# A one-core RWKV-7 / HGRN2 / pooling block: queue places of the solver, of the transpositions and of the first weights, five staging buffers for the output weights, and another order of the last HGRN steps

## The chip, the cores and the metric

The program runs on one core of a Trainium2 chip. It computes one layer of a hybrid backbone over 2048 latent tokens and 256 context tokens, all in float32. The metric is the device time of one execution in microseconds (us), from the kernel's first to its last instruction; times of a kernel are the median of its runs.

The engines are PE (TensorE, matrix products), DVE (VectorE), ACT (ScalarE), POOL (GpSimd) and SP (SyncE, which here only issues DMAs). Each engine takes its instructions in one fixed order. An instruction whose input is not there holds everything behind it on that engine.

## The reference, cut to what matters

```python
p_lat = (_layer_norm(h_x) * (1.0 + sc_l[:, None]) + sh_l[:, None]) @ w_in[l]
p_ctx = (_layer_norm(h_ctx) * (1.0 + sc_c) + sh_c) @ w_in[l]
pv_l, u_l, fh_l, g_l = _split_proj(p_lat)
...
y_rc, y_rl = _rwkv_branch(u_c, u_l, ...)
o_hc, o_hl = _hgrn_branch(fh_c, fh_l, ...)
pool_l = _pool_branch(pv_l, True, pool_w[l], pool_scale[l])
mix_l = jnp.concatenate([pool_l, y_rl, o_hl], axis=-1) * jax.nn.silu(g_l)
new_x = _layer_norm(ALPHA * h_x + gt_l[:, None] * (mix_l @ w_out[l])) * ln_g[l] + ln_b[l]
```

RWKV is a recurrence over tokens in two directions (the state is multiplied by a decay, loses its part along one key and gains an outer product). HGRN is a gated recurrence over tokens in two directions. Each branch is gated by SiLU of its own part of the input projection; the output projection merges them.

## The kernel before, in words

**Stages.** First come the layer norm and the projections that RWKV needs (until about 490 us). Then three things run one behind the other, with the remaining input projections threaded through them as filler for PE: RWKV (about 550 to 1335 us), HGRN (about 1335 to 1834 us) and the readout with the output projection (to the end).

**The filler** is the generator `filler` (lines 537 to 593). For each of three parts of 768 tokens it loads the activations `fxs`/`fxl` (line 542), splits them into a high and a low half (`split`, lines 213 and 214: a cast on ACT to `fxh`, a subtraction on DVE to `fxl`), and then goes over 22 blocks of 128 output columns. For each block `weights` (line 563) loads 512 KB into `fwf` (line 217, one buffer, SP's queue), casts it on ACT to `fwh` (line 213) and subtracts on POOL to `fwl` (line 214). 24 matmuls per group of tokens (line 583) follow: eight of (fxh, fwh), eight of (fxh, fwl), eight of (fxl, fwh). A group's `sink` takes the result away; its second half (`rest`: for the pooling blocks the product of line 642) is run inside the next group, after its 18th matmul (line 587).

**RWKV** goes over 36 chunks of 64 tokens in both directions. Chunk n's triangular systems are set up by `start` (matmuls of line 738, masks of line 740 on DVE), collected by `gather` (lines 778 to 780), and solved for four chunks together by `solve` (lines 784 to 803): 31 pairs of a multiplication (line 795, tile `tm`) and a subtraction (line 798, tile `o`), all on DVE. `merge` (lines 822 to 861) fetches the solution (`nn`, `at`), transposes it on DVE (lines 839 and 842) and multiplies on PE (line 847). `step` does the recurrence itself; its new state `zbd` is made on DVE by lines 903 (`tz`) and 905 from the matmuls of line 899. So DVE has four kinds of work in one queue: masks, transpositions, states, and the solver. The order on PE is written by hand in the loop of lines 960 to 991 (under `manual_schedule`); the order on the other engines, SP's queue among them, is set by a scheduler from that program.

**HGRN** goes over windows of 256 tokens, one of context and eight of latents, with a slot table (line 1167). In window n the *levels* of window n (line 1061 on PE, line 1090 on DVE for `qp` and on POOL for `ks`) alternate with the *steps* of window n−1 (lines 1120, 1123, 1133 on PE, and the state `sbd` by line 1138 on DVE, six of it per step). After the last levels one window holds steps alone. The weights of the output projection are loaded there too (`out_weights`, lines 1146 to 1158): eight pieces of 384 KB into the one `fwf`, multiplied on POOL by the gate (line 1153), cast on ACT, subtracted on DVE (line 214).

**The readout** (lines 1231 to 1287) loads `ya`, `yb`, `oa`, `ob` and, for the pooled channels, `gt` and `mx` (lines 1236 to 1255), adds on POOL (lines 1251 and 1259), multiplies `mx` on DVE (line 1256), splits it into `mh` (ACT, line 1243) and `ml`, and normalises `ya` by a chain of DVE and ACT operations (lines 1261 to 1265). PE's output projection starts with `mh` (line 1300); PE's transposes of `ya` (line 1274) come next in its order.

## Time and profile before

| what | value |
|---|---|
| median of 3 runs | 2080.55 us (2076.18 to 2083.02) |
| the profiled execution | 2072.91 us, span of its trace 2070.8 us |
| PE busy | 1835.0 us, 89% of the span |
| DVE busy | 1435.9 us, 69% |
| ACT, POOL busy | 922.4 us (45%), 796.9 us (38%) |
| chain that ended last | PE 50%, DVE 19%, DMA 7%, issue 4%, ACT 2%, POOL 2% |

The span is that of one execution. The chain that ended last is followed back from the last instruction, at each step to whatever released it. The busy shares are means over stages with different limits, so each stage is read by itself, and in it the idle time of PE and what ended it.

### The profile page before, as it was taken

How to read it: one execution, taken by the hardware profiler on the slowest of the kernel's cores; microseconds unless marked ns; L12 is line 12 of the kernel's file. 1: busy time of each engine (PE TensorE's matmuls, PEld its weight loads, DVE VectorE, ACT ScalarE, POOL GpSimd, SP SyncE). 2: the span in 40 equal slices, each digit the busy share in tenths (PEclk: the TensorE clock that was granted, in tenths of full speed). 3: DMA queues.
4: the chain of work that ended last, by engine and by line, in shares of the span. 5: the costliest groups of instructions: out<-in, count | busy, mean ns of one | idle time of the engine just before them, and what ended most of it. 6: DMA issues, size and time to landing. Idle time of an engine off the chain costs nothing.

```text
span 2070.8 us, 47037 instructions
## 1 busy us (share of the span) xinstructions
PE 1835.0 (89%) x18498; PEld 1556.3 (75%) x18498; DVE 1435.9 (69%) x3040; ACT 922.4 (45%) x1759; POOL 796.9 (38%) x735
## 2 busy tenths in 40 slices
PE   5698899994898898999988897989999999869898
PEld 2687788884786677787777786877778778758887
DVE  3778889997047857846766756258778888669863
ACT  4876777664222342332333234355456555222331
POOL 0144345655321233232223222354345553434753
PEclk8899899997899999999999999999999999659999
DMA  8444444435555576565655655443233332176632
GB/s 305 157 147 136 134 127 123 123 100 177 156 168 145 159 230 182 158 175 154 176 153 152 169 144 161 136 138 109 79 101 103 110 91 85 55 262 194 215 133 74
DMA packets 286452, 305.32 MB, mean 147 GB/s; under 512 B 85076, under 2 KB 244948, under 8 KB 285208
## 3 DMA queue, kind: packets, MB, share of 16 engines
q1 hardware_dynamic: 276072, 271.64, 43.7%
q10 hardware_dynamic: 5040, 18.09, 2.6%
q0 software_dynamic: 5120, 12.59, 1.9%
q8 instruction: 146, 2.39, 0.5%
q14 instruction: 74, 0.61, 0.1%
HBM read 205.49 MB, written 96.74 MB: 146 GB/s over the span
## 4 chain that ended last, share of the span: by engine, by line
PE 50%; DVE 19%; DMA 7%; issue 4%; ACT 2%; POOL 2%; SPq 1%; DVEq 0%; ACTq 0%; POOLq 0%
PE fps L583 18%; PE ps L332 3%; PE pa L1061 3%; PE po L1300 2%; DVE tm L795 2%; PE pa L738 2%; DVE o L798 2%; PE pa L874 2%; PE pa L1123 2%; PE pa L1120 2%; PE pa L880 2%; DVE sbd L1138 2%; PE pa L890 2%; PE po L1304 1%; PE po L1302 1%
## 5 line engine op out<-in xcount | busy, mean ns | idle before, releaser
L214 POOL TENSOR_TENSOR fwl<-fwf,fwh 128x1024 fp32r<-128x1024 f32 x66 | 158.8, 2407 | 360.7 <-ACT fwh L213 338.9
L583 PE MATMUL fps<-fxh,fwh 128*128 128x256 f32 (+1 forms) x952 | 224.7, 371 | 24.6 <-ACT fwh L213 17.0
L583 PE MATMUL fps<-fxl,fwh 128*128 128x256 f32 (+1 forms) x952 | 219.8, 364 | 1.3 <-DVE fxl L214 1.3
L583 PE MATMUL fps<-fxh,fwl 128*128 128x256 f32 (+1 forms) x952 | 212.5, 355 | 1.9 <-POOL fwl L214 1.9
L583 PEld LDWEIGHTS fps<-fxh,fwh 128*128 128x128 f32 x952 | 156.9, 197 | 54.3 <-ACT fwh L213 19.0
L583 PEld LDWEIGHTS fps<-fxl,fwh 128*128 128x128 f32 x952 | 160.7, 198 | 29.5 <-issue 5.6
L583 PEld LDWEIGHTS fps<-fxh,fwl 128*128 128x128 f32 x952 | 155.9, 193 | 28.2 <-POOL fwl L214 3.0
L1138 DVE SCALAR_TENSOR_TENSOR sbd<-sbd,tot,pa 64x64 f32<-64x64 f32 x432 | 120.6, 279 | 37.8 <-PE pa L1133 27.7
L920 POOL TENSOR_TENSOR ys<-ys,pp 64x384 f32<-64x384 f32 x64 | 75.0, 1172 | 186.2 <-ACT ys L917 176.1
L1056 ACT COPY qb<-qp 64x384 f32<-64x384 f32 x192 | 99.9, 520 | 100.4 <-PE pa L1061 67.6
L795 DVE TENSOR_TENSOR tm<-m,o 96x31 f32<-96x31 f32 (+15 forms) x279 | 114.7, 411 | 39.2 <-DMA m<-sd 31.3
L332 PE MATMUL ps<-xh,wh 128*128 128x258 f32 x768 | 129.0, 309 | 6.4 <-DVE t L337 4.4
L740 DVE TENSOR_TENSOR at<-pa,cst 128x384 f32<-128x384 f32 x144 | 74.1, 548 | 82.9 <-PE pa L738 82.3
L798 DVE TENSOR_TENSOR o<-o,tm 96x31 f32<-96x31 f32 (+15 forms) x279 | 120.4, 432 | 7.9
L332 PEld LDWEIGHTS ps<-xh,wh 128*128 128x128 f32 x768 | 108.7, 203 | 20.4 <-issue 7.8
L332 PE MATMUL ps<-xh,wl 128*128 128x258 f32 x768 | 119.7, 297 | 0.0
L1090 POOL TENSOR_TENSOR ks<-ks,tot 128x384 f32<-128x384 f32 x90 | 86.8, 969 | 84.7 <-PE pa L1061 74.2
L332 PE MATMUL ps<-xl,wh 128*128 128x258 f32 x768 | 116.4, 291 | 1.6 <-DVE xl L322 1.6
L332 PEld LDWEIGHTS ps<-xh,wl 128*128 128x128 f32 x768 | 106.8, 201 | 4.7 <-issue 4.3
L332 PEld LDWEIGHTS ps<-xl,wh 128*128 128x128 f32 x768 | 103.3, 194 | 5.1 <-issue 3.0
L1061 PE MATMUL pa<-qb,ks 128*64 128x64 f32 x2304 | 92.5, 233 | 6.9 <-POOL ks L1090 3.5
L412 POOL TENSOR_TENSOR kr<-t 128x256 f32<-128x256 f32 x54 | 47.1, 871 | 130.0 <-ACT t L399 65.1
(233 smaller groups left out, 4351.9 us busy)
## 6 DMA issues: line engine op xcount, KB each, us to landing
fwf<-in_w_in_dram SPq DMA_DIRECT2D x66, 512.0 KB, 4.4
xt<-in_x_dram ACTq DMA_DIRECT2D x32, 512.0 KB, 4.3
s_kr<-kr SPq DMA_DIRECT2D x54, 256.0 KB, 2.3
s_bk<-bk SPq DMA_DIRECT2D x54, 256.0 KB, 2.4
bks<-s_bk SPq DMA_DIRECT2D x72, 192.0 KB, 3.0
krs<-s_kr SPq DMA_DIRECT2D x72, 192.0 KB, 3.2
bk<-s_bk SPq DMA_DIRECT2D x72, 192.0 KB, 3.0
kr<-s_kr SPq DMA_DIRECT2D x72, 192.0 KB, 3.8
```

What stands on the lines that cost most here:

```text
L214: eng.tensor_tensor(out=wl, in0=wf, in1=wh.bitcast(F32), op=ALU.subtract)
L332: PE.matmul(ps[:, 0:TG + 2], a[:, k, :], b[:, k, :], start=(i == 0), stop=(i == 23))
L412: G.tensor_tensor(out=kr[:, :, pr], in0=c4(kk), in1=e_k, op=ALU.mult)
L583: PE.matmul(ps[:, 0:n], a[:, k, :], b[k][:, o:o + n], start=(i == 0), stop=(i == 23))
L740: V.tensor_tensor(out=at[:, h], in0=pa[h], in1=cst[:, C_MASK[d]].unsqueeze(1).broadcast_to([P, NPR, P]), op=ALU.mult)
L795: V.tensor_tensor(out=tv, in0=m[:, j:j + 1, j + 1:32].broadcast_to([nrow, na, nb]), in1=o[:, 0:na, j:j + 1].broadcast_to([nrow, na, nb]), ...
L798: V.tensor_tensor(out=o[:, 0:na, j + 1:32], in0=o[:, 0:na, j + 1:32], in1=tv, op=ALU.subtract)
L920: G.tensor_tensor(out=ys[vr], in0=ys[vr], in1=pp[d][vr], op=ALU.add)
L1056: S.copy(out=qb[hh, :, :, h, :].rearrange("q p c (i b) -> q (p c) i b", b=b), in_=src[hh].rearrange("q p (c i j b) -> q (p c) i j b", c=nc ...
L1061: PE.matmul(pl[64 * (c % 2):64 * (c % 2) + 64, :, p, c // 2, :], ks[:, p, CH * c:CH * c + CH], qb[:, p, c, :, :], start=True, stop=True)
L1090: eng.tensor_tensor(out=v_, in0=v_, in1=tv[:, :, :, 1 - par:2 - par].broadcast_to([P, NPR, nb, b]), op=ALU.mult)
L1138: V.scalar_tensor_tensor(out=sn[hh, p, hh], in0=so_[hh, p, hh], scalar=tot[hh, p, c:c + 1], in1=ps[hh, p, :], op0=ALU.mult, op1=ALU.add)
```

## The change

It edits the filler, the RWKV loop, the staging of the output weights and the HGRN slots. Lines shift by 1 to 13.

- `weights` leaves the loop over the parts. The first block's weights are issued ahead of the first activations, and the first weights of the second and third part are fetched at the end of the part before. `rest` runs behind all 24 matmuls of the next group, not behind the 18th.
- `gate["v"]` names the newest mask or state on DVE. Pieces of the solver and the transpositions of `merge` are put into the program with `issue_after(gate)`: the scheduler places them behind that instruction. `merge` and `solve` yield after their loads; merge's loads are put to the start of an iteration, and a solver's load to the end of the iteration that gathers its fourth chunk.
- `out_weights(0)` rotates over `fwf`, two `fwh` and two `fwl`, five buffers in all.
- In the window with steps alone the directions alternate (s0, s1, s0, s1) where before each took two in a row. In the window before it, the filler is paced to slot 7, and the output weights are run two per slot from there.

```diff
+        nxt = weights(blocks[0][0])
         xs = ahead(parts[0])
...
-                if bi + 1 < len(blocks):
-                    nxt = weights(blocks[bi + 1][0])
+                if bi + 1 < len(blocks) or pi + 1 < len(parts):
+                    nxt = weights(blocks[(bi + 1) % len(blocks)][0])
...
-                                if i == 18:
-                                    run(rest)
+                        run(rest)
                         rest = sink(fp, side["ps"], sl, n, ps[:, 0:n])
...
-                    V.tensor_tensor(out=at[:, h], in0=pa[h],
+                    gate["v"] = V.tensor_tensor(out=at[:, h], in0=pa[h],
                                     in1=cst[:, C_MASK[d]].unsqueeze(1).broadcast_to([P, NPR, P]), op=ALU.mult)
...
             G.memset(o.rearrange("q a t -> q (a t)")[:, 0:32 * 32:33], -1.0)
+            yield 1
...
                 ws[n][d]["uv"] = uv
+            yield 1
...
-                    V.tensor_tensor(out=zn[d].rearrange("q p (h e) -> q p h e", h=2), in0=tz,
+                    gate["v"] = V.tensor_tensor(out=zn[d].rearrange("q p (h e) -> q p h e", h=2), in0=tz,
...
-                            go("sol", g, solve, k)
+                            with tc.issue_after(gate["v"].ins):
+                                go("sol", g, solve, k)
                 go("stp", n, step)
                 go("late", n + 1, late)
+                go("mer", n + 1, merge)
...
-                go("mer", n + 1, merge)
+                with tc.issue_after(gate["v"].ins):
+                    go("mer", n + 1, merge)
...
+                if s_ % SB == SB - 1:
+                    go("sol", s_ // SB, solve)
                 beside(n, 0.22)
...
-                wf = fp.tile([P, KB, P], F32, name="fwf").rearrange("q k c -> q (k c)")[:, 0:n]
+                nm0, bufs, dt = (("fwf", 1, F32), ("fwh", 2, F32R), ("fwl", WB, F32R))[k % 3 if j == 0 else 0]
+                wf = fp.tile([P, KB, P], dt, name=nm0, bufs=bufs)
+                wf = (wf if dt is F32 else wf.bitcast(F32)).rearrange("q k c -> q (k c)")[:, 0:n]
...
-                for si, slot in enumerate(slots):
+                for si, slot in enumerate(slots if n < nw else slots[:4] + ("s0", "s1") * 4):
...
-                    if n < nw - 1:
+                    if n < nw - 1 or n == nw - 1 and si < 7:
                         pace(H_FIL[0] if n == 0 else H_FIL[1] if n < 3 else H_FIL[2])
                     elif n == nw - 1:
-                        run(fill if si == 0 else ow, None if si == 0 else 1)
+                        if si == 7:
+                            run(fill)
+                        run(ow, 2)
```

Three places show what the scheduler makes of it. A row is one instruction, or several alike in a row, as they stand on their engine.

The first place is SP's queue where the filler's first loads stand. Before, the first load of weights (`fwf`) comes behind the last activations (`fxs`) and four loads for RWKV:

```order
181 L542 DMA fxs<-s_x 128x256
182 L542 DMA fxs<-s_x 128x512
183 L542 DMA fxs<-s_x 128x256
184 L725 DMA bks_6005<-s_bk 128x384
185 L726 DMA krs_6004<-s_kr 128x384
186 L725 DMA bks_6010<-s_bk 128x384
187 L726 DMA krs_6009<-s_kr 128x384
188 L542 DMA fxs<-s_x 128x512
189 L217 DMA fwf<-in_w_in_dram 128x1024
190 L725 DMA bks_6253<-s_bk 128x384
```

In the change, still among the stores of the stage before (`s_kr`, `s_bk`, `s_vt`) and ahead of the first activations:

```order
147 L423 DMA s_kr<-kr 128x4x128
148 L424 DMA s_bk<-bk 128x4x128
149 L390 DMA s_vt<-t 128x2x128
150 L423 DMA s_kr<-kr 128x4x128
151 L217 DMA fwf<-in_w_in_dram 128x1024
152 L423 DMA s_kr<-kr 128x4x128
153 L424 DMA s_bk<-bk 128x4x128
154 L390 DMA s_vt<-t 128x2x128
155 L440 DMA s_bon<-t 128x256
156 L542 DMA fxs<-s_x 128x256
```

The load went up by all of the 24 loads of activations; the second load of weights now stands right behind them (its row is 185).

The second place is DVE in chunk 10, the second iteration of the solver of chunks 12 to 15. `tm` and `o` are the solver, `at` from `pa` the masks, `zbd` the state. Before, the transpositions (L842) stand ahead of this piece, and seven solver operations stand between `o` 96x18x14 and the first mask:

```order
1185 L798 TENSOR_TENSOR o<-o,tm 96x18x14
1186 L795 TENSOR_TENSOR tm<-m,o 96x247
1187 L798 TENSOR_TENSOR o<-o,tm 96x19x13
1188 L795 TENSOR_TENSOR tm<-m,o 96x240
1189 L798 TENSOR_TENSOR o<-o,tm 96x20x12
1190 L795 TENSOR_TENSOR tm<-m,o 96x231
1191 L798 TENSOR_TENSOR o<-o,tm 96x21x11
1192 L795 TENSOR_TENSOR tm<-m,o 96x220
1193 L740 TENSOR_TENSOR at_9626<-pa,cst 128x384
1194 L798 TENSOR_TENSOR o<-o,tm 96x22x10
1195 L740 TENSOR_TENSOR at_9626<-pa,cst 128x384
```

In the change, the masks first:

```order
1181 L799 TENSOR_TENSOR o<-o,tm 96x18x14
1182 L740 TENSOR_TENSOR at_9636<-pa,cst 128x384
1183 L796 TENSOR_TENSOR tm<-m,o 96x247
1184 L740 TENSOR_TENSOR at_9636<-pa,cst 128x384
1185 L799 TENSOR_TENSOR o<-o,tm 96x19x13
```

and from the state to the transpositions:

```order
1189 L905 TENSOR_TENSOR tz_9991<-pa,zbd_5980 128x384
1190 L905 TENSOR_TENSOR tz_9994<-pa,zbd_5982 128x384
1191 L799 TENSOR_TENSOR o<-o,tm 96x21x11
1192 L907 TENSOR_TENSOR zbd_5981<-tz_9991,dms_5988 128x384
1193 L907 TENSOR_TENSOR zbd_5983<-tz_9994,dms_5989 128x384
1194 L841 STREAM_TRANSPOSE nn<-nn 32x192
1195 L844 STREAM_TRANSPOSE at_8105<-nn 32x6x32 x2
```

The first mask moved ahead of seven solver operations, the state too, and the three transpositions now stand directly behind the state.

The third place is the end of HGRN. On DVE before, where `sbd_16240` and `sbd_16241` are direction 0 and `sbd_16242` and `sbd_16243` direction 1, the last steps come in pairs of one direction, with the subtractions of the output weights (`fxl`) between them and `mx` behind all:

```order
2195 L1138 SCALAR_TENSOR_TENSOR sbd_16241<-sbd_16240,tot_21669,pa 64x64 x6
2196 L1138 SCALAR_TENSOR_TENSOR sbd_16240<-sbd_16241,tot_21669,pa 64x64 x6
2197 L1138 SCALAR_TENSOR_TENSOR sbd_16243<-sbd_16242,tot_21689,pa 64x64 x6
2198 L214 TENSOR_TENSOR fxl_21465<-fwf,fxh_21464 128x768
2199 L1138 SCALAR_TENSOR_TENSOR sbd_16242<-sbd_16243,tot_21689,pa 64x64 x6
2200 L1138 SCALAR_TENSOR_TENSOR sbd_16241<-sbd_16240,tot_21669,pa 64x64 x6
2201 L214 TENSOR_TENSOR fxl_21515<-fwf,fxh_21514 128x768
2202 L1138 SCALAR_TENSOR_TENSOR sbd_16240<-sbd_16241,tot_21669,pa 64x64 x6
2203 L1138 SCALAR_TENSOR_TENSOR sbd_16243<-sbd_16242,tot_21689,pa 64x64 x6
2204 L1138 SCALAR_TENSOR_TENSOR sbd_16242<-sbd_16243,tot_21689,pa 64x64 x6
2205 L1256 TENSOR_TENSOR mx<-mx,gt 128x512
```

On DVE in the change:

```order
2182 L1097 TENSOR_TENSOR qp_21075<-qp_21075,tot_21649 128x12x32
2183 L1269 TENSOR_TENSOR mx<-mx,gt 128x512
2184 L1145 SCALAR_TENSOR_TENSOR sbd_16243<-sbd_16242,tot_21132,pa 64x64 x6
2185 L1070 COPY_PREDICATED sc_21074<-cst,pa 128x24x16
2186 L1145 SCALAR_TENSOR_TENSOR sbd_16242<-sbd_16243,tot_21132,pa 64x64 x6
2187 L1070 COPY_PREDICATED sc_21080<-cst,pa 128x24x16
2188 L1070 COPY_PREDICATED sc_21074<-cst,pa 128x12x32
2189 L1070 COPY_PREDICATED sc_21080<-cst,pa 128x12x32
2190 L1145 SCALAR_TENSOR_TENSOR sbd_16241<-sbd_16240,tot_21669,pa 64x64 x6
2191 L1145 SCALAR_TENSOR_TENSOR sbd_16243<-sbd_16242,tot_21689,pa 64x64 x6
2192 L1145 SCALAR_TENSOR_TENSOR sbd_16240<-sbd_16241,tot_21669,pa 64x64 x6
2193 L1145 SCALAR_TENSOR_TENSOR sbd_16242<-sbd_16243,tot_21689,pa 64x64 x6
```

The directions alternate from row 2190, no subtraction of weights is left among them, and both `mx` moved up into the last window of levels. On POOL, in that window, the change has the readout's two additions among the `ks` of the levels, where before they came behind the last of them:

```order
561 L1097 TENSOR_TENSOR ks_20812<-ks_20812,tot_21241 128x192x2
562 L1163 TENSOR_TENSOR fwf<-fwf,gtb 128x768
563 L1097 TENSOR_TENSOR ks_20800<-ks_20800,tot_21284 128x96x4
564 L1135 DMA s_o<-os 128x384
565 L1097 TENSOR_TENSOR ks_20812<-ks_20812,tot_21329 128x96x4
566 L1264 TENSOR_TENSOR ya<-ya,yb 128x1536
567 L1097 TENSOR_TENSOR ks_20800<-ks_20800,tot_21372 128x48x8
568 L1135 DMA s_o<-os 128x384
569 L1272 TENSOR_TENSOR oa<-oa,ob 128x1536
570 L1097 TENSOR_TENSOR ks_20812<-ks_20812,tot_21417 128x48x8
```

Both additions wait for their loads, and five `ks` stand behind the second.

## Rows read from the trace of the kernel before

**Rows 1.** Busy time, last stage: us, PE, PEld, DVE, ACT, POOL, PEclk, DMA, GB/s.

```profile
1760.00:2071.00 311.00, 266.82 (x1973) 235.16 (x1970) 215.66 (x336) 82.72 (x125) 152.54 (x77) 0.84 0.46 155
```

**Rows 2.** Timeline of SP's queue: start us, us, engine, line, operation.

```profile
513.72 0.40 SPq L217 DMA_DIRECT2D fwf<-in_w_in_dram  x1
```

**Rows 3.** Timeline of ACT, 513 to 521 us; brackets: idle before, what ended it.

```profile
513.38 0.83 ACT L213 CAST fxh<-fxl 128x768 fp32r<-128x768 f32 x1 [0.56 <-DMA fxl<-s_x]
519.56 1.04 ACT L213 CAST fwh<-fwf 128x1024 fp32r<-128x1024 f32 x1 [5.35 <-DMA fwf<-in_w_in_dram]
```

**Rows 4.** Timeline of PE, 520 to 537 us: the filler's first blocks.

```profile
520.65 3.78 PE L583 MATMUL fps<-fxh,fwh 128*128 128x512 f32 x8 [15.05 <-ACT fwh L213]
...
529.45 2.11 PE L583 MATMUL fps<-fxh,fwh 128*128 128x512 f32 x8 [0.43 <-ACT fwh L213]
...
536.57 2.11 PE L583 MATMUL fps<-fxh,fwh 128*128 128x512 f32 x8 [0.73 <-ACT fwh L213]
```

**Rows 5.** Timeline of PE in chunks 10 and 26 of RWKV.

```profile
869.96 1.64 PE L738 MATMUL pa<-krs,bks 64*128 64x128 f32 x10 [5.10 <-DVE at L740]
...
874.39 0.58 PE L847 MATMUL pa<-nn,at 32*32 32x32 f32 x24
...
1187.97 1.64 PE L738 MATMUL pa<-krs,bks 64*128 64x128 f32 x10 [5.69 <-DVE at L740]
```

**Rows 6.** Timeline of DVE in chunk 10.

```profile
862.00 0.78 DVE L842 STREAM_TRANSPOSE at<-nn 32x192 f32<-32x192 f32 x2
...
864.62 0.42 DVE L798 TENSOR_TENSOR o<-o,tm 96x252 f32<-96x252 f32 x1
...
869.36 0.55 DVE L740 TENSOR_TENSOR at<-pa,cst 128x384 f32<-128x384 f32 x1
...
873.23 1.01 DVE L905 TENSOR_TENSOR zbd<-tz,dms 128x384 f32<-128x384 f32 x2
```

**Rows 7.** Busy time by stretch, columns as in rows 1: chunk 10 and HGRN's end.

```profile
1765.34:1796.06 30.72, 30.41 (x312) 25.79 (x312) 22.92 (x53) 8.20 (x15) 10.37 (x11) 0.50 0.17 56
1796.06:1809.71 13.65, 9.11 (x160) 7.78 (x158) 7.84 (x18) 3.86 (x7) 8.10 (x7) 1.00 0.13 44
...
867.60:874.40 6.80, 4.44 (x24) 3.99 (x24) 6.56 (x18) 0.00 (x0) 0.88 (x2) 0.50 0.23 50
```

**Rows 8.** Timeline of PE in HGRN: the first line waits for the pooling blocks' scans.

```profile
1506.62 2.08 PE L642 MATMUL pa<-fe,pw 128*128 128x512 f32 x2 [3.33 <-DVE fe L639]
```

**Rows 9.** Timeline of SP's queue at HGRN's end.

```profile
1763.68 55.57 SPq L1152 DMA_DIRECT2D fwf<-in_w_out_dram  x6
1819.46 0.38 SPq L1236 DMA_DIRECT2D ya<-s_y  x1
```

**Rows 10.** Timeline of PE from HGRN's last steps into the readout.

```profile
1803.86 0.91 PE L1120 MATMUL pa<-it,sc 64*64 64x64 f32 x12
...
1809.65 1.94 PE L1123 MATMUL pa<-sbd,qp 128*64 128x128 f32 x6 [3.06 <-DVE sbd L1138]
...
1832.67 0.91 PE L1133 MATMUL pa<-it,kt 64*64 64x64 f32 x12
1841.48 0.80 PE L1300 MATMUL po<-fxh,mh 128*128 128x512 f32 x1 [7.90 <-ACT mh L1243]
...
1855.36 2.79 PE L1274 MATMUL pg<-cst,ya 128*128 128x128 f32 x12 [9.83 <-DVE ya L1265]
```

**Rows 11.** Timeline of POOL in the readout.

```profile
1832.53 3.41 POOL L1251 TENSOR_TENSOR ya<-ya,yb 128x1536 f32<-128x1536 f32 x1 [4.66 <-DMA yb<-s_y]
...
1836.77 3.40 POOL L1259 TENSOR_TENSOR oa<-oa,ob 128x1536 f32<-128x1536 f32 x1 [0.32 <-DMA ob<-s_o]
```

**Rows 12.** Timeline of DVE in the readout.

```profile
1838.04 2.69 DVE L1256 TENSOR_TENSOR mx<-mx,gt 128x512 f32<-128x512 f32 x1 [2.57 <-DMA mx<-s_pool]
...
1842.07 0.68 DVE L1256 TENSOR_TENSOR mx<-mx,gt 128x512 f32<-128x512 f32 x1
...
1844.05 1.74 DVE L1261 TENSOR_REDUCE mu<-ya 128x24 f32<-128x1536 f32 x1
```

14 lines of the change are left out of this document (7 added, 7 removed).

## The prediction, made before the change was run

> **What bounds the kernel now.** First I read the busy shares: PE works 89% of the span, so time is lost where PE stands idle or runs at a lower clock. Then I took PE's timeline stage by stage, noted each idle time with what ended it, and kept those that the change can reach. They lie in four places. At the filler's start PE is idle 15.05 us for the first weights [rows 4]; ACT waits 5.35 us for a load that SP issued only at 513.72 [rows 2, 3]. In RWKV PE waits at line 738 for masks that stand on DVE behind solver operations; six such waits, four of them of 4.3 to 5.7 us, sum to 21.8 us; the first and the last are in [rows 5]. In HGRN it waits 3.33 us for a pooling block [rows 8]. At the end PE is busy 267 of 311 us at 0.84 of full clock [rows 1]; it waits 3.06 us for a state, 7.90 us for `mh` and 9.83 us for `ya` [rows 10], and SP's queue stands 55.57 us with six loads of output weights that wait for one buffer, `ya` behind them [rows 9].
>
> **The sum** is made against the profiled execution, 2072.91 us. The median of the runs, 2080.55, is 7.6 us (0.37%) above it; I add that at the end.
>
> **First weights: −8.** Before, the first load takes 513.72 to 519.56, 5.8 us with its wait, and blocks start at 520.65, 529.45 and 536.57 [rows 2 to 4]. In the changed order the load stands ahead of all activations and is long done. The first block then waits for the last cast of activations, 513.38 + 0.83 = 514.2. Its last matmul of the first eight follows, 0.5 us, then what lay between the first eight and the second block before: 529.45 − (520.65 + 3.78) = 5.0 us. That is 519.7. The second load, now directly behind the activations, is issued about when the first was, lands at 519.6 like it and is cast by 520.6. So the second block starts near 520.6 and not at 529.45: −8.9. Blocks after that are 7.12 us apart either way. The first load's 512 KB now lies ahead of the activations. If they came later by its whole 5.8 us, 3 us would be left; ACT's last wait for them is 0.56 us, so the queue is not the tight place there, and I take 0.9 off. Bounds −3 and −9. Moving the RWKV loads behind the second weights costs nothing: their matmuls come 30 us later.
>
> **RWKV's DVE order: −2.** I worked out chunk 10. Before, the transpositions end at 862.78, solver operations follow, and the first mask comes at 869.36 [rows 6]; PE resumes 5.10 us late [rows 5]. Now seven of these operations, from 864.62 + 0.42 = 865.04 to 869.36, so 4.3 us, stand behind the mask, and the transpositions, 0.78 for two and so 1.2 us for three, come later as well. With 4.3 + 1.2 = 5.5 us less ahead of it, the mask moves to 863.9, before PE had to stop at 869.96 − 5.10 = 864.9: −5.1. What is late next is line 847. PE would reach it at 874.39 − 5.10 = 869.3. From 863.9 DVE has two masks (1.1), six of the seven operations (3.8), `tz` and `zbd` (2.0, as `zbd` alone takes 1.01 for two) and the transpositions (1.2): 872.0. So PE waits 2.7 us there, and the chunk gains 2.4. Four such chunks give −10. Against that, eighteen chunks run beside a solver (nine solvers, two iterations each), and in the other fourteen the 1.2 us of transpositions now lie between the state and line 847, where before they lay ahead. At most that is 14 × 1.2 = 17; a part falls into room that PE's filler leaves, and I count half, 0.6 each: +8. The solver's own 62 operations stay; with DVE full while it runs, they are only late elsewhere. Bounds: −22 (all six waits gone, no new ones) and +17 (no wait gone, all transpositions seen). I take −2, by chunk 10 and the count. The loads of a solver and of `merge`, put earlier in the program, I cost at nothing: in SP's order they moved by a few rows, and they wait for the stores that they read.
>
> **Pooling blocks in HGRN: −2.** The product of line 642 now comes six matmuls later. Six of the filler's matmuls are 2.11 × 6/8 = 1.6 us at 512 columns [rows 4] and half of it at 256. Two waits of over 2 us stand there, the longer of 3.33 [rows 8]; each loses about 1 us. Bounds 0 and −3.2.
>
> **The last HGRN window: −5.** It runs from 1803.86 to 1832.67 + 0.91 = 1833.58 [rows 10], 29.7 us for eight steps. Where one direction takes two steps in a row, the second needs the state that DVE has just begun to make; PE stood 3.06 us and then ran at half clock until the end of the window: the granted clock was 1.00 up to 1809.71 [rows 7], and matmuls of line 1123 after it took 1.94 for six. Alternating takes this wait away, since the other direction's matmuls lie between: −3.1. It is open whether the clock then stays at 2.4 GHz. For it: the wait came right before the fall. Against it: from 1765.34 PE ran 30.7 us at 0.50 with hardly an idle moment, on the same kinds of matmuls [rows 7]. If it stays: at full clock the first step and the next one's first group took 1809.65 − 3.06 − 1803.86 = 2.7 us, so eight steps of at most 2.35 are 19 us, −11. If it falls as before, −3. I take −5, nearer to the second.
>
> **Readout: −7.5.** The six weight loads no longer wait for one buffer, so `ya`, `yb`, `gt` and `mx` land and both additions are done before the steps end. What then stands behind the last step is: `mh` and `ml` (1841.48 before, now 2.5 us after the last step) and the chain from the reduction at 1844.05 [rows 12] to line 1274 at 1855.36 [rows 10], 11.3 us, which still waits in DVE's queue behind the last states. So line 1274 comes 2.5 to 3 + 11.3 = 14 to 14.3 us after the last step, and before it was 1855.36 − 1833.58 = 21.8. That is −7.5. Bounds −6.5 and −8.5.
>
> **POOL and DVE in the last window of levels: +2.** Both additions, 3.41 and 3.40 us [rows 11], and the two `mx` now stand among the levels, where `ks` on POOL and states on DVE queue behind them. They wait for loads of 768 KB; in the readout POOL stood idle 4.66 us for `yb` [rows 11]. PE runs at half clock there, DVE is busy 22.9 of 30.7 us and POOL 10.4 [rows 7], so most fits. Bounds 0 and 3.41 + 3.40 = 6.8. On DVE, the trace shows `mx` at 2.69 us beside the addition of `oa`, and at 0.68 alone [rows 11, 12]. The Trainium skill, on its page "SBUF — State Buffer", section "Who interferes with whom", states that a VectorE instruction with two SBUF inputs and a GpSimd instruction that reads SBUF exclude each other for the whole instruction. By that rule, which the row bears out (2.69 against 0.68), each addition stops DVE up to its whole length, and I would put 6.8 here instead of 2.
>
> **Sum:** −8 − 2 − 2 − 5 − 7.5 + 2 = −22.5; 2072.9 − 22.5 = 2050.4, and on the scale of the median **2058 us**.
>
> **The rivals.** About 0.3%, 6.2 us, is what a measurement of this kernel tells from no change: faster is below 2074.3, slower above 2086.8.
>
> *Masks free and clock high.* All six waits for masks go without new ones, RWKV −22, and the last window stays at full clock, −11. Sum −48.5: 2032. For it: behind such a wait PE runs at half clock for a while (0.50 from 867.6 to 874.4 [rows 7]), which would go too. Against it: DVE's full queue.
>
> *The additions block the levels.* `ks`, `qp` and the states wait 6.8 us on top of the 2 for additions, loads and `mx`: sum −15.7, 2065. For it speaks the row of 2.69; against it PE's slow clock in that window. It is what the rule of the page "SBUF — State Buffer" of the Trainium skill would do here.
>
> *RWKV's waits only move.* All fourteen transpositions are seen in full (+17) and the masks gain 4 instead of 10: RWKV +13, sum −7.5, 2073. For it: the solver's work is conserved and DVE has no idle time in chunk 10; against it: the first mask really stands earlier.
>
> *Line 847 becomes the wait of every solver chunk (slower).* The transpositions stand behind `zbd` and `zbd` behind line 899, so line 847 waits for a chain of DVE's in-order queue that was not there. If each of the eighteen chunks waits 2.7 us as chunk 10 does, and the masks keep their waits because the solver's operations are only pushed together: +49 − 20.5 = +28, 2109. It decides from 1.5 us per chunk (−20.5 + 18 × 1.5 = +6.5). For it: it was computed so for chunk 10. Against it: chunk 10 is the second iteration of a solver, where the queue is fullest; in the first ones the state itself stands earlier than before.
>
> That RWKV's order changes nothing gives −20.5, inside my forecast.
>
> **How the numbers follow.** Forecast 0.50, masks and clock 0.17, blocked levels 0.10, waits that only move 0.10, line 847 slower 0.13. Of the forecast 0.45 is below 2074.3 and 0.05 above; of blocked levels 0.09 and 0.01; of waits that move 0.03 and 0.07. So faster 0.17 + 0.45 + 0.09 + 0.03 = 0.74, the same 0.13, slower 0.13. The forecast's own range is 2044 to 2073 (bounds of the terms, not all at one end). The range goes from 2031 to 2085: it leaves out the slower rival and the lower half of the first, 0.2 together.
>
> **What would show it.** First block's idle before line 583 ended by `fxh`, second block near 521. Line 738 of chunk 10 without its 5 us, line 847 with about 2.7 us for DVE. L1152's stall on SP gone, `ya` issued before 1790, line 1274 14 us behind the last step. The window with steps alone under 27 us; its clock tells −3 from −11. I am wrong if PE's idle time in front of line 847 sums to more than 25 us, or if POOL's `ks` in the last window of levels start behind a waiting `ya`.

## The result and the profile after

The change takes **2059.18 us** (median of 4 runs, 2054.41 to 2063.67), the kernel before, run beside it, 2081.78 us (4 runs, 2076.18 to 2089.58): a ratio of 0.9886, 95% interval 0.9854 to 0.9918. That is faster by more than the 0.3% set as the bound, and 1.2 us from the forecast of 2058. The profiled execution of the change took 2062.20 us, that of before 2072.91.

The total was right; several of its terms were not. This table sets the predicted terms beside the profiles. Each row is the growth or loss of one stage against the profile of before, read from the start of PE's marker matmuls: line 899 (901) of RWKV's chunk 0, the first matmul of each half of a latent window's levels on line 1061 (1068), counted 0 to 15 ("level 12" is the mark with this number), steps on line 1133 (1140), and line 1274 (1287). The second profile is of another run of the same kernel.

| stage, us | predicted | change | change again |
|---|---|---|---|
| up to chunk 0 of RWKV (first weights) | -8 | -3.3 | -5.9 |
| RWKV, to the first level of HGRN | -2 | -8.3 | -2.3 |
| HGRN, levels 0 to 8 (pooling blocks) | -2 | -2.6 | -4.6 |
| levels 8 to 10 | 0 | +4.7 | +4.0 |
| level 10 to the end of the levels | +2 | +19.7 | +17.9 |
| steps alone | -5 | -13.9 | -13.9 |
| last step to line 1274 | -7.5 | -9.1 | -8.9 |
| rest of the readout | 0 | +2.3 | +6.0 |
| sum | -22.5 | -10.5 | -7.7 |

The profiled sums are smaller than the difference of the medians (22.6 us), because the profiled execution of before is 8.9 us under the median given here and that of the change 3.0 us over its own. Part of this can be placed: the kernels below that leave the staging alone also lose 4.9 to 5.8 us from level 8 to 10 against the profile of before, and about 1.4 from level 11 to 12. So before's profiled execution was a quick one there, by some 6 us.

Single rows must be read with the same care, since kernels that are alike in a stage still differ there. In RWKV, alternation alone and the staging run below are the kernel before, and take 4.7 and 4.5 us more than its profile. The change, its second profile and three edits of its end (`mx` late, additions late, staging held back) have the change's RWKV, and stand at -8.3, -2.3, -5.0, -12.4 and -5.1 us. Their rows on DVE, POOL and SP are the same there. So one profile against another shows no difference of under 5 to 10 us in this stage.

**The filler's start** after, PE's timeline (start, duration, engine, line, operation, out<-in, shape, count, and in brackets the idle time before with what ended it):

```profile
512.17 0.80 PE L583 MATMUL fps<-fxh,fwh 128*128 128x512 f32 x1 [1.87 <-ACT fxh L213]
514.92 0.80 PE L583 MATMUL fps<-fxh,fwh 128*128 128x512 f32 x1 [1.95 <-ACT fxh L213]
521.38 1.98 PE L583 MATMUL fps<-fxh,fwh 128*128 128x512 f32 x8
532.51 2.08 PE L583 MATMUL fps<-fxh,fwh 128*128 128x512 f32 x4 [5.53 <-ACT fwh L213]
```

and SP's queue in the same stretch:

```profile
512.77 0.43 SPq L217 DMA_DIRECT2D fwf<-in_w_in_dram  x1
513.25 0.90 SPq L752 DMA_DIRECT2D kr<-s_kr  x2
...
523.84 1.09 SPq L829 DMA_DIRECT2D uv<-s_vt  x2
525.03 0.53 SPq L217 DMA_DIRECT2D fwf<-in_w_in_dram  x1
```

Against [rows 4], PE no longer stands 15.05 us: the first block comes with the activations, each wait ended by `fxh`, and the second block is at 521.38, where 520.6 to 521 was forecast. But the third is at 532.51 and no longer 7.12 us behind the second: PE waits 5.53 us for `fwh`. The third load of weights is issued at 525.03, behind fourteen rows (18 loads) for RWKV on SP. Before, fourteen such loads stood between the first load of weights and the second (513.72 to 523.70), and none between the second and the third.

**RWKV**: PE's line 738 and line 847 (849) by source, before and after. The lines in the middle say how long PE stood idle before this line, how often, and what ended it. Before:

```profile
L738 PE MATMUL pa<-krs,bks x768: 271/272/577, 605.5 to 1224.5; 64*128 64x128 f32 x192
  DVE at L740: 21.8, 6
```

```profile
L847 PE MATMUL pa<-nn,at x840: 190/191/258, 647.3 to 1317.8; 32*32 32x32 f32 x168
  DVE nn L839: 11.7, 2
  DMA nn<-so: 4.0, 3
```

After (line 738 has no such line any more):

```profile
L849 PE MATMUL pa<-nn,at x864: 184/191/258, 641.4 to 1322.7; 32*32 32x32 f32 x173
  DVE nn L841: 44.0, 14
  DMA nn<-so: 7.5, 5
```

All six waits for masks are gone, the waits ahead of the pooling blocks' line 642 (641) fell from 15.9 us to 2.6, and those ahead of line 847 (849) grew from 15.7 us to 51.5. In all PE stood 725.00 - 648.00 = 77.0 us in this stretch before and 71.5 after:

```profile
605.00:1330.00 725.00, 648.00 (x7983) 0.95 0.58 163
```

```profile
605.00:1330.00 725.00, 653.49 (x8052) 0.94 0.59 165
```

(columns: stretch, its length, PE's busy time and instructions, granted clock, share and GB/s of the DMA engines). Chunk 10 on DVE, which the prediction worked out, shows the order that was forecast, masks, tz, state and transpositions (the two masks at 864.93 are the next pair):

```profile
856.87 0.55 DVE L740 TENSOR_TENSOR at<-pa,cst 128x384 f32<-128x384 f32 x1
...
857.66 0.55 DVE L740 TENSOR_TENSOR at<-pa,cst 128x384 f32<-128x384 f32 x1
...
861.14 1.01 DVE L905 TENSOR_TENSOR tz<-pa,zbd 128x384 f32<-128x384 f32 x2
862.07 0.39 DVE L799 TENSOR_TENSOR o<-o,tm 96x231 f32<-96x231 f32 x1
862.38 1.02 DVE L907 TENSOR_TENSOR zbd<-tz,dms 128x384 f32<-128x384 f32 x2
863.42 0.37 DVE L841 STREAM_TRANSPOSE nn<-nn 32x192 f32<-32x192 f32 x1
863.82 0.77 DVE L844 STREAM_TRANSPOSE at<-nn 32x192 f32<-32x192 f32 x2
864.62 0.38 DVE L796 TENSOR_TENSOR tm<-m,o 96x220 f32<-96x220 f32 x1
864.93 1.01 DVE L740 TENSOR_TENSOR at<-pa,cst 128x384 f32<-128x384 f32 x2
```

PE then waits 3.90 us at line 849 (2.7 were forecast) and none at line 738.

**The end of HGRN**, PE by stretches. After:

```profile
1760.00:1803.00 43.00, 36.51 (x447) 0.68 0.54 187
1803.00:1814.10 11.10, 7.62 (x102) 0.69 0.41 138
1814.10:1829.60 15.50, 15.46 (x241) 1.00 0.11 38
1829.60:1842.60 13.00, 3.75 (x12) 0.55 0.77 265
```

Eight steps now take 15.5 us at full clock; before it was 29.7 at a mean of 0.60 ([rows 10] have its first and last matmul). Behind them PE waits for `ya` as before, but line 1287 starts at 1842.63, 13.1 us behind the last step (1829.55), where it was 21.8; 14 to 14.3 were forecast. SP's stall of [rows 9] is gone: `ya` is issued at 1785.30, before 1790 as forecast. What was not forecast stands just before the steps, on PE, DVE and POOL:

```profile
1806.02 1.94 PE L1130 MATMUL pa<-sbd,qp 128*64 128x128 f32 x6 [5.29 <-DVE sbd L1145]
```

```profile
1798.90 4.91 DVE L1269 TENSOR_TENSOR mx<-mx,gt 128x512 f32<-128x512 f32 x1 [1.57 <-DMA mx<-s_pool]
1804.78 0.69 DVE L1269 TENSOR_TENSOR mx<-mx,gt 128x512 f32<-128x512 f32 x1
1805.38 1.84 DVE L1145 SCALAR_TENSOR_TENSOR sbd<-sbd,tot,pa 64x64 f32<-64x64 f32 x6
```

```profile
1793.39 3.44 POOL L1264 TENSOR_TENSOR ya<-ya,yb 128x1536 f32<-128x1536 f32 x1 [5.92 <-DVE qp L1097]
1796.78 0.87 POOL L1097 TENSOR_TENSOR ks<-ks,tot 128x384 f32<-128x384 f32 x1
...
1798.19 3.44 POOL L1272 TENSOR_TENSOR oa<-oa,ob 128x1536 f32<-128x1536 f32 x1
1801.58 1.67 POOL L1097 TENSOR_TENSOR ks<-ks,tot 128x384 f32<-128x384 f32 x2
```

One `mx` multiplication of DVE takes 4.91 us where its twin takes 0.69. It begins 0.7 us after POOL's addition of `oa`, and ends 0.56 us after the two `ks` behind that addition. The state of line 1145 is queued behind it, PE waits 5.29 us for the state.

### The profile page after: what moved, and what is told of

Read it like the earlier page. It is cut to its first block, busy times and chain, and to the rows that moved or that the text cites. A ratio compares the mean times of both kernels' runs of the same rounds, so it can differ in the third digit from the quotient of the medians.

```text
span 2060.4 us, 47040 instructions
## 1 busy us (share of the span) xinstructions
PE 1838.5 (89%) x18498; PEld 1560.0 (76%) x18498; DVE 1441.4 (70%) x3040; ACT 921.0 (45%) x1759; POOL 801.4 (39%) x735
## 4 chain that ended last, share of the span: by engine, by line
PE 35%; DVE 25%; DMA 8%; issue 5%; ACT 3%; POOL 2%; SPq 1%; ACTq 0%; DVEq 0%; POOLq 0%
PE fps L583 14%; DVE o L799 4%; DVE tm L796 4%; PE po L1313 2%; PE pa L1068 2%; DVE sbd L1145 2%; PE pa L876 1%; DVE tot L1100 1%; PE po L1315 1%; PE po L1317 1%; DVE at L740 1%; PE pa L882 1%; DVE ml L1257 1%; PE pa L1130 1%; DMA so<-o 1%
## 5 line engine op out<-in xcount | busy, mean ns | idle before, releaser
L583 PE MATMUL fps<-fxh,fwh 128*128 128x256 f32 (+1 forms) x952 | 232.4, 378 | 18.2 <-ACT fe L598 7.6
L583 PE MATMUL fps<-fxh,fwl 128*128 128x256 f32 (+1 forms) x952 | 219.1, 364 | 0.6 <-POOL fwl L214 0.6
L583 PE MATMUL fps<-fxl,fwh 128*128 128x256 f32 (+1 forms) x952 | 211.0, 356 | 0.0
L583 PEld LDWEIGHTS fps<-fxh,fwl 128*128 128x128 f32 x952 | 161.7, 199 | 27.7 <-POOL fwl L214 0.8
L1145 DVE SCALAR_TENSOR_TENSOR sbd<-sbd,tot,pa 64x64 f32<-64x64 f32 x432 | 120.6, 279 | 41.2 <-PE pa L1140 30.8
L799 DVE TENSOR_TENSOR o<-o,tm 96x31 f32<-96x31 f32 (+15 forms) x279 | 115.3, 413 | 8.3
```

The lines of the kernel that those rows point to most:

```text
L583: PE.matmul(ps[:, 0:n], a[:, k, :], b[k][:, o:o + n], start=(i == 0), stop=(i == 23))
L799: V.tensor_tensor(out=o[:, 0:na, j + 1:32], in0=o[:, 0:na, j + 1:32], in1=tv, op=ALU.subtract)
L1145: V.scalar_tensor_tensor(out=sn[hh, p, hh], in0=so_[hh, p, hh], scalar=tot[hh, p, c:c + 1], in1=ps[hh, p, :], op0=ALU.mult, op1=ALU.add)
```

## The experiments

Ratios are to the kernel before, run on the same chip in the same job, with 95% intervals. In the first job it took 2084.80 us, in the second 2079.08, in the third 2083.58.

### One part of the change at a time

The first four runs put single parts of the diff shown above into the kernel before.

Not run alone were the pooling blocks' `rest` behind the 24th matmul, and staging without the paced filler.

**First weights alone:** the weights of the first block ahead of the activations, those of the next part fetched across the border.

```diff
+        nxt = weights(blocks[0][0])
...
-                if bi + 1 < len(blocks):
-                    nxt = weights(blocks[bi + 1][0])
+                if bi + 1 < len(blocks) or pi + 1 < len(parts):
+                    nxt = weights(blocks[(bi + 1) % len(blocks)][0])
```

> The kernel before, with the early first weights and the fetch across part borders alone. Theory A (each part acts in its own stage, the gains add): the second block of the filler starts 8 us earlier as in the change, but the third only 4 us earlier, because its weights are loaded behind thirteen RWKV loads on SP; time -3 to -6 us. Rival B (RWKV behind it is bound by DVE and by its own loads, and absorbs a head start): 0 +- 2 us by the first chunks of RWKV. Rival C (the forecast's term): -8 us kept to the end.

Measured: 2068.34 us, 0.9915 (0.9889 to 0.9941). The second, third and fourth block start 11.5, 9.3 and 9.4 us earlier than before, RWKV's chunk 0 is 10.7 us earlier. Of this 2.9 us are no gain of the edit: the stage ahead of the filler, which is the same in both kernels, ended that much earlier in this execution. What is left, 7.9 us, is what the forecast's term promised; that the third block would gain only 4 us was wrong. The gain in time, 0.85% or some 18 us, is more than twice that, and the profile does not show where the rest comes from.

**RWKV's order alone:** `gate`, the two `yield 1`, and the moved loads of `merge` and of the solver.

```diff
+                            with tc.issue_after(gate["v"].ins):
+                                go("sol", g, solve, k)
...
+                go("mer", n + 1, merge)
...
+                with tc.issue_after(gate["v"].ins):
+                    go("mer", n + 1, merge)
```

> The kernel before, with the gates, the yields and the moved loads of solver and merge alone. Theory A: the waits at line 738 (21.8 us) go, waits at line 847 come, net -4 to -10 us at the end of RWKV, as the change's trace shows -7 there (chunk 0 to chunk 34). Rival B (RWKV gives the whole gain of the change, the tail none): -18 to -22 us. Rival C (the solver's work is only pushed together): 0 +- 3 us.

Measured: 2074.81 us, 0.9975 (0.9944 to 1.0006). From chunk 0 to chunk 34 it gains 4.6 us in the profile. PE waits 52.6 us ahead of the line of the transpositions, as in the change, and none for masks. The profile bears out the first theory; on the time, this part can't be told from no change.

**Staging, pacing and alternation:**

```diff
+                nm0, bufs, dt = (("fwf", 1, F32), ("fwh", 2, F32R), ("fwl", WB, F32R))[k % 3 if j == 0 else 0]
...
+                for si, slot in enumerate(slots if n < nw else slots[:4] + ("s0", "s1") * 4):
...
+                    if n < nw - 1 or n == nw - 1 and si < 7:
```

> The kernel before, with five staging buffers, the paced filler in the last window of levels and the alternating steps. Theory A: readout -8, steps -3 (clock falls) to -14 (clock stays), last levels +4 to +8 from mx and the two additions: -5 to -15 us in sum. Rival B (mx and the additions among the levels eat what staging gives): 0 +- 3 us.

Measured: 2062.64 us, 0.9916 (0.9884 to 0.9949); its profiled execution, 2078.82 us, was the slowest of its 12 runs. The gain, some 18 us by the ratio, is more than the 5 to 15 that were expected.

**Alternation alone:**

```diff
-                for si, slot in enumerate(slots):
+                for si, slot in enumerate(slots if n < nw else slots[:4] + ("s0", "s1") * 4):
```

> The kernel before, with the alternating steps alone; the weights still wait for one buffer, and their subtractions lie among the steps. Theory A: the 3.06 us wait of line 1123 goes and the granted clock stays at 1.00 through the steps: the window from 29.7 to 16-19 us, but the readout still waits for the last weights, which then come after the steps, so only -2 to -5 us remain at line 1274. Rival B: the clock falls without the wait, too: window 26 us, and nothing remains at line 1274. Rival C: steps are what bounds the end: -11 us remain.

Measured: 2079.03 us, 0.9967 (0.9936 to 0.9998). The steps alone shrink by 4 us, from 27.2 to 23.0 between the first and the last of them, where staging, pacing and alternation together give 13.2. PE still waits 1.23 us for a state behind the second step and goes on at half clock, and line 1274 stands as far behind the last step as before: the second theory comes nearest.

The three parts alone are worth 0.85%, 0.25% and 0.84%, 1.9% if they added; the change has 1.1%. With the intervals of all four taken as independent, the 0.8% that are missing are an estimate of 0.2 to 1.4%. So the parts seem to hinder each other. In the first weights this can't be shown (next section); in the levels, 11 to 12 takes 27.9 or 28.0 us with each part alone and 34.6 and 30.9 in the change's two profiles.

### The third load of weights

Is it really the queue on SP that eats the first weights' gain? RWKV's first loads (scores of chunks 0 and 1, `late` and `merge` of chunk 0) are put behind the third load of weights:

```diff
+            with tc.issue_after(wdma[2].ins):
+                go("sc", 0, start)
...
-                go("late", n + 1, late)
-                go("mer", n + 1, merge)
+                with tc.issue_after(wdma[2].ins) if n < 1 else ExitStack():
+                    go("late", n + 1, late)
+                    go("mer", n + 1, merge)
```

> The change, with the RWKV loads of chunks 0 and 1 put behind the third load of weights on SP. Theory A (in the change the third block is late because thirteen RWKV loads stand ahead of its weights): the third load is issued near 522.5 instead of 525.0 and lands sooner, the third block starts at 527 to 528 instead of 532.5, chunk 0's line 901 comes 5 to 8 us earlier than in the change, and the time is 4 to 8 us below the change's, if RWKV keeps it. Rival B (RWKV is bound by its own loads at the start, which come later now): chunk 0 no earlier, time unchanged within 2 us. Rival C (the solvers absorb it): earlier at chunk 0, gone by chunk 8.

The same job ran the change once more, as its yardstick:

> The change as it is, beside the next three. Theory A (the half clock of HGRN's fifth to seventh window in its first trace, which cost it 13 us between chunks of levels, comes and goes by run): the time in that stretch differs, the waits elsewhere come back: line 738 without the 5 us, line 849 with 4 to 6 us in second iterations of a solver, the state before the last steps 5 us late behind mx. Rival B (the change causes the half clock there): the stretch is slow again. Ratio to before 0.989 either way.

Measured: the change 2061.15 us, 0.9897 (0.9851 to 0.9942); with the edit 2054.92 us, 0.9861 (0.9811 to 0.9911). The second profile of the change is slow again from level 10 (+17.9 us), so that its rival holds better than its first theory, though level 11 to 12 is 3.7 us shorter. With the edit SP issues the third load 5.4 us earlier:

```profile
519.67 0.33 SPq L217 DMA_DIRECT2D fwf<-in_w_in_dram  x1
```

The third block starts at 525.06, 11.5 us earlier than before, and chunk 0 is 9.4 us earlier, as with the part alone. So loads for RWKV on SP's queue do hold up the third load of weights. But they are not the change's own doing: with the first weights alone, SP's rows from the first load of weights to the fourth are the same, row by row, with the same eighteen loads in the way:

```profile
509.70 0.43 SPq L217 DMA_DIRECT2D fwf<-in_w_in_dram  x1
...
520.98 0.53 SPq L217 DMA_DIRECT2D fwf<-in_w_in_dram  x1
```

And most of the 9.4 us are there without this edit. The next table counts from the end of the last matmul of line 332 (333), the stage ahead of the filler, which no edit touches and which ended between 483.2 and 489.6 us in these profiles.

| kernels, us | third load behind second | third block | chunk 0 |
|---|---|---|---|
| before and three without early weights | 8.0 to 8.2 | 49.7 to 50.8 | 178.3 to 179.6 |
| first weights alone | 11.3 | 43.4 | 171.1 |
| the change; its second profile | 12.3; 12.5 | 45.5; 44.7 | 175.5; 172.9 |
| four runs below with the change's rows here | 11.3 to 12.6 | 43.1 to 45.4 | 171.1 to 175.6 |
| RWKV's loads behind the third load (three runs) | 8.4 to 9.2 | 39.5 to 40.1 | 170.8 to 172.0 |

The edit brings the third load forward by 2 to 4 us and the third block by 3 to 6, clear of the spread. At chunk 0 its three runs are on average 2.2 us ahead of the six with the change's rows, and the ranges overlap. The intervals of the two times overlap too.

### The additions and mx in the last window of levels

Two edits take the long `mx` away from DVE's queue. The first puts the two `mx` multiplications on DVE behind the last state; the second puts both additions of the first readout behind the last `ks` on POOL, and `mx` on POOL as well.

```diff
-                V.tensor_tensor(out=mx, in0=mx, in1=gt, op=ALU.mult)
+                with tc.issue_after(last["s"].ins) if g == gs[0] else ExitStack():
+                    V.tensor_tensor(out=mx, in0=mx, in1=gt, op=ALU.mult)
```

> The change, with the two multiplications of mx on DVE put behind the last state; both additions stay among the levels on POOL. Theory A (mx, waiting for its load and then shut out by the addition on POOL, makes the state of line 1145 late: 5.29 us of PE's time): that wait goes, PE's idle time before the last window falls by 4 to 5 us; the readout starts 1.5 to 2.5 us later behind the last step. Net -2 to -4 us against the change. Rival B (the additions among the ks are the cause): the wait before line 1130 stays over 3 us.

```diff
+            early = g == gs[0]
+            with tc.issue_after(last[True].ins) if early else ExitStack():
+                G.tensor_tensor(out=ya, in0=ya, in1=yb, op=ALU.add)
...
+                    (G if early else V).tensor_tensor(out=mx, in0=mx, in1=gt, op=ALU.mult)
```

> The change, with both additions put behind the last ks on POOL, and the two multiplications of mx moved from DVE to POOL behind the first addition. Theory A: no wait for a state or for ks in the last levels beyond the 2.5 us at their start; the additions and mx are done during the steps (about 10 us of POOL, steps 15 us), so the readout starts no later: -5 to -8 us against the change. Rival B (what PE gains there is lost behind the last step, because POOL is not done in time): L1313 over 3 us behind the last step and no gain.

Measured: 2051.04 us, 0.9855 (0.9809 to 0.9901), and 2051.09 us, 0.9855 (0.9811 to 0.9899). Both medians are 10 us under the change in the same job, with overlapping intervals. The stage tells more than the time. From level 15 to the first step alone the change takes 25.6 us (26.2 in its other profile, 25.0 with the third load moved), with `mx` late 24.4, and with the additions late **18.3**. PE over this stage, in the change, with `mx` late and with the additions late:

```profile
1790.11:1815.76 25.65, 19.90 (x267) 0.74 0.68 239
```

```profile
1790.59:1815.03 24.44, 23.57 (x267) 0.58 0.67 230
```

```profile
1775.85:1794.14 18.29, 17.68 (x267) 0.81 0.61 221
```

With `mx` late the wait for the state falls from 5.29 us to 0.6, as expected, but little time is won, since PE then runs at a lower granted clock (0.58, with the additions late 0.81). Nor is DVE free: the next multiplication in its queue takes the place of `mx`. It is `qp`, 0.58 us in the median of the last windows, here beside the addition of `oa` (1798.69 to 1802.12) and two `ks` (to 1803.75):

```profile
1798.50 5.67 DVE L1098 TENSOR_TENSOR qp<-qp,tot 128x384 f32<-128x384 f32 x1
```

So the additions on POOL are what stops DVE, not the place of `mx`, and the 7.3 us between the change and the additions late are 5.1 us of PE's idle time and the rest clock. They are not all kept: with the additions late line 1274 (1287) starts 17.5 us behind the start of the last step's state matmuls, and not 13.6, as the rival for that run feared in part.

### Both edits, the staging held back, and the transpositions not held

The last job combined the two edits that gained (third load, additions behind `ks`), tested the staging, and took one order of RWKV away. For the second question, POOL's multiplication of each piece of the output weights is put behind the newest `ks`:

```diff
+                with tc.issue_after(last[True].ins) if j == 0 else ExitStack():
                     G.tensor_tensor(out=wf, in0=wf, in1=gtb[:, c], op=ALU.mult)
```

> The change, with the gate's multiplication of each of the eight 768-column pieces of the output weights ordered behind the last ks multiplication of HGRN that stands before it in the program, so none of them runs on POOL beside the levels of the last window but one. Theory (those pieces beside DVE are what lengthens that window): from the tenth level marker to the thirteenth PE loses under 4 us against the kernel before, where the change lost 10 to 13, and if the last window can take the 8 x 1.82 = 15 us of POOL's work the time is 2050 to 2056. Rival 1 (PE's clock falls there for another reason): the loss stays at 10 us or more and the time is the change's within 3 us. Rival 2 (the work only moves): the stretch is regained, but the last levels grow by as much or more, since the ks multiplications then queue behind the pieces on POOL, and the time is 2060 to 2070.

> The change with both edits that gained alone: RWKV's first loads queued on SP behind the third load of the first weights, and the additions and the two mx multiplications of the first readout on POOL behind the last ks. If the two are independent (prologue and last levels) their gains add: 6 and 10 us under the change, 2045, a ratio of 0.982 to the kernel before. If one of them owed its gain to where the clock fell, 2050 or the same as the better one alone. Markers: third block of the prologue 9 to 12 us earlier than before, steps of the last window without a wait over 2 us for the mx multiplication.

The third run has both edits and this one:

> The same with the multiplications of the output weights held back as well. By the theory that these pieces lengthen the last window but one: 5 to 8 us under the run with the two edits, 2037 to 2042. By the rival that the work only moves into the last levels: as much as the run with the two edits, or 5 us above it.

Measured: staging held back 2071.70 us, 0.9939 (0.9909 to 0.9968), some 10 us above the change's medians, with intervals that just overlap; both edits 2064.52, 0.9901 (0.9876 to 0.9927), and not the 2045 of gains that add; all three 2062.72, 0.9892 (0.9863 to 0.9922), and not 2037 to 2042. Stage lengths in the profiles, us between markers:

| kernel | 8 to 10 | 11 to 12 | 12 to 13 | 14 to 15 | 15 to steps | steps |
|---|---|---|---|---|---|---|
| before | 48.6 | 26.5 | 21.4 | 26.8 | 21.4 | 27.2 |
| RWKV's order alone | 53.5 | 27.9 | 21.3 | 22.8 | 18.6 | 27.3 |
| alternation alone | 53.5 | 27.9 | 21.4 | 26.9 | 23.3 | 23.0 |
| first weights alone | 54.3 | 28.0 | 21.3 | 23.0 | 30.8 | 26.0 |
| staging, pacing, alternation | 53.0 | 27.9 | 27.2 | 28.2 | 22.0 | 13.2 |
| change | 53.3 | 34.6 | 26.3 | 29.4 | 25.6 | 13.2 |
| change again | 52.5 | 30.9 | 27.3 | 29.6 | 26.2 | 13.2 |
| additions late | 53.7 | 34.2 | 27.5 | 28.4 | 18.3 | 13.2 |
| both edits | 53.6 | 34.6 | 27.4 | 28.2 | 18.2 | 13.2 |
| staging held back | 52.6 | 26.9 | 26.3 | 16.1 | 36.1 | 23.6 |
| all three | 53.5 | 34.5 | 27.2 | 16.1 | 34.8 | 23.6 |
| transpositions not held | 52.9 | 27.9 | 27.5 | 28.4 | 24.1 | 13.2 |

Three readings. *First*, the stage 12 to 13 takes 21.3 to 21.4 us with one staging buffer and 26.3 to 27.6 with five, whether POOL's pieces stand there or not. (No run has the five buffers without the paced filler and the alternation, so it could be any of the three.) So my theory that these pieces lengthen this window fell. What all kernels with five buffers share is a later `f`: ACT begins on its first load 6.2 to 7.2 us after level 12 and not 5.5 to 5.7, although SP issues its load 2.2 us after that level in all of them. DVE's `tot` and state come later by that, PE waits 1.2 to 3.3 us once and goes on at half clock. Why ACT gets this load later is open; no run tried it. *Second*, the pieces had to go somewhere. Held back, they leave level 14 to 15 at 16.1 us, at full clock, and then stand with their loads among the last `ks` on POOL:

```profile
1782.68 2.17 POOL L1165 TENSOR_TENSOR fwh<-fwh,gtb 128x768 f32<-128x768 f32 x1 [4.14 <-DMA fwh<-in_w_out_dram]
...
1793.90 1.80 POOL L1165 TENSOR_TENSOR fwf<-fwf,gtb 128x768 f32<-128x768 f32 x1 [6.85 <-DMA fwf<-in_w_out_dram]
1795.66 0.84 POOL L1098 TENSOR_TENSOR ks<-ks,tot 128x384 f32<-128x384 f32 x1
```

POOL waits 6.85 us for a load, `ks` waits behind it, and PE stands 8.51 us for that `ks`. That is the rival written for this run, that the work only moves: 12 us are regained, more than that is lost. *Third*, where PE stood that long right before them, the steps run at half clock (23.6) although they alternate and PE does not wait in them:

```profile
1797.00:1830.00 33.00, 29.81 (x248) 0.50 0.62 206
```

The two edits that gained alone do not add in the time: their run is level with the change. In its profile they keep the stages where they act, 18.2 us before the steps, and RWKV's chunk 0 7.3 us earlier than before by the count of the table above. Against that, line 1287 stands 18.0 us behind the last step and not 13.6, and level 11 to 13, where PE's clock falls, takes 62.1 us (the change 60.8 and 58.2, before 48.0). The better times of the single edits are therefore not shown to be theirs.

Last, the change without the order of `merge` behind the masks:

```diff
-                with tc.issue_after(gate["v"].ins):
-                    go("mer", n + 1, merge)
+                go("mer", n + 1, merge)
```

> The change without the order of RWKV's merge behind the masks of its solver: the transpositions may again stand ahead of the masks on DVE's and PE's queues. Theory (the gate trades one wait for another): waits ahead of line 738 of about 5 us come back in some chunks, those of 2 to 6 us ahead of line 849 go, and the border of RWKV moves by under 4 us either way; time within 4 us of the change. Rival (the gate is what gives back 9 us in the last solver and at the border): the waits ahead of 849 go, those ahead of 738 do not come back, and the border is 5 to 9 us earlier: 2052 to 2056.

Measured: **2049.02 us, 0.9826 (0.9801 to 0.9852)**, the fastest of all. Its interval lies below those of the other three of its job; against the change's two, measured in other jobs, it ends just below the one (from 0.9854) and just meets the other (from 0.9851). PE's waits change back as the theory said:

```profile
L738 PE MATMUL pa<-krs,bks x744: 272/272/579, 613.1 to 1216.0; 64*128 64x128 f32 x186
  DVE at L740: 15.8, 8
```

```profile
L849 PE MATMUL pa<-nn,at x864: 184/191/258, 642.8 to 1324.5; 32*32 32x32 f32 x173
  DVE nn L841: 6.4, 3
  DMA nn<-so: 5.3, 4
```

```profile
605.00:1330.00 725.00, 658.59 (x8036) 0.94 0.58 164
```

PE's idle time in RWKV falls to 725.00 - 658.59 = 66.4 us, 5 under the change (in its second profile it was 67.4), but RWKV as a whole gains 8.1 us, as in the change's first profile (8.3). So the profile does not find the 12 us between the medians in RWKV. It finds 6 to 8 of them from level 10 to the steps: most from level 11 to 12 (27.9 us against 34.6 and 30.9), where the order on every engine is the same in both kernels, and some 2 us behind level 15, where one state stands ahead of a masked copy and the second `mx` on DVE and not behind them, since the scheduler orders everything anew. From level 11 to 12 the granted clock was 0.94, and 0.70 and 0.83 in the change. The theory (within 4 us of the change) fell with the time, the rival with the waits; how much of the gain belongs to the gate is open.

## Why the prediction was right, and where it was not

**The number and the direction** were right: 2059.18 against 2058. That they agree to 1.2 us is luck. In the profiles the gain of the steps was far larger than its term, the loss in the levels far larger than its own, and the sum is -10.5 and -7.7, not -22.5; only the medians, of which before's is 8.9 us above its profile, differ by 22.6.

**First weights, -8.** The mechanism held to the second block (521.38). "Blocks after that are 7.12 us apart either way" and "Moving the RWKV loads behind the second weights costs nothing" are the step that failed: not RWKV's matmuls need those loads early, but the third load of weights stands behind them, and the third block came 11.13 us behind the second. Moving them away gave 3 to 6 us at the third block and some 2 at chunk 0. Counted from the stage ahead, chunk 0 gained 3.5 us in the change, 6.1 in its second profile, and 3.4 to 7.9 in the five other profiles with the same rows on SP, so the size of the term held within its bounds.

**RWKV, -2.** The profiles gain 8.3 and 2.3 us, the part alone 4.6 from chunk 0 to 34 and not measurably on the time. Given the spread of this stage that says little more than that the size lay within its wide bounds. The working did not: I wrote that I am wrong if PE's idle time before line 847 sums to more than 25 us, and it is 51.5. The first half of the slower rival came true, (51.5 - 15.7) / 18 chunks = 2.0 us each, above its deciding point of 1.5. Its second half did not: the masks kept none of their 21.8 us, and 13.3 of 15.9 us before the pooling blocks' line 642 went too. The wait changed its line, as the run without the order of `merge` shows from the other side.

**Pooling blocks, -2:** the two waits fell from 2.54 and 3.33 us to 1.82 and 1.32, in every kernel with this edit, together 2.7 us. The stage's -2.6 shows less, since alternation alone, without the edit, has -3.1 there.

**Steps, -5:** -13.9; I chose the wrong side of an open question. The bound for a clock that stays, -11, had 2.35 us per step; measured are 13.2 / 7 = 1.9. Alternation alone leaves most of the stage at half clock (23.0), behind a wait of 1.23 us for a state; only together with the new staging and pacing is it 13.2.

**Readout, -7.5:** -8.7 by its own working (13.1 against 21.8), 0.2 us beyond its bound; the mechanism held. The rest of the readout, +2.3 and +6.0, had no term.

**POOL and DVE in the last window, +2.** This is the term that was mis-sized most. Additions and `mx` cost 25.6 - 18.3 = 7.3 us before the steps, above my upper bound of 6.8, since I let PE's slow clock cover them; 3.8 of these come back at line 1287 when the additions stand later, so that in these profiles their place costs the kernel some 3.5. The Trainium skill, on its page "SBUF — State Buffer", section "Who interferes with whom", lets a VectorE instruction with two SBUF inputs and a GpSimd instruction that reads SBUF exclude each other; by it I would have put 6.8, and the trace agrees: `mx` at 4.91 us ends only after the addition and two `ks`, against 0.69 alone. The rest of the +19.7 had no term at all: 8.0 us from level 11 to 12 (4.4 in the second profile), where every engine's order is that of the run without the order of `merge` (27.9 us) and the clock is lower; 4.8 and 5.9 from 12 to 13; 2.5 and 2.8 from 14 to 15, where the kernel with its staging held back takes 13 us less. I had costed the extra buffers where they free SP, not where their loads and products land. The second criterion, `ks` behind a waiting `ya`, holds in part: `ks` starts at 1796.78, right behind the addition's 3.44 us, but the addition's own idle time was ended by DVE's `qp`, not by its load.

## What to carry to other kernels

When a load is moved up, list what it passes and what it is put in front of: here the loads that stood ahead of the second weights came to stand ahead of the third, and held them up by 2 to 4 us. And before a gain is read from two profiles, count from an event that no edit touches: here the stage ahead of the edit ended some 6 us apart. An order that takes away a wait on an engine that is full gives it to the next consumer on that engine; look at PE's idle time over the whole stage, not at the line. And a long addition on POOL placed "in the shade" beside DVE's two-input operations is paid in DVE's queue, by whichever of them comes next: count its whole length.

## What the runs showed of the hardware

- DVE's `mx`, 128x512 with two inputs in SBUF, took 4.91 us beside POOL's addition and two multiplications that followed it without a pause, and 0.69 alone: it did not get in between them. With `mx` out of the way, `qp` (128x384, two inputs in SBUF) took 5.67 us in the same place, 0.58 in the median.
- The same eight steps ran at a granted clock of 1.00 (15.5 us) 8 us of matmuls after a wait of PE of 5.29 us, and at 0.50, 4 us of matmuls after a wait of 8.51 us. PE did not wait within the steps in either, so the clock was set by what stood before them. Short waits were followed by half clock as well: the single waits of 1.2 to 3.3 us at level 12 to 13, and the one of 1.23 us in the steps of alternation alone.
- The same program varies by about 0.5% to either side from run to run (2049.33 to 2067.89 us in six runs of the change). Its two profiles differ by 6.0 us in RWKV and by 3.7 from level 11 to 12 (34.6 at a granted clock of 0.70, 30.9 at 0.83), although the spans are 2.8 us apart.
